# A decoder trunk whose transposes of FFN activations and residual chunks move from TensorE to VectorE and a trip through DRAM

## The chip, the cores and the metric

The kernel runs on 1 core of one Trainium2 chip. The metric is the device time of one execution in microseconds (us), lower is better; each time given for the kernel is the median of several runs. The profile is one further execution, taken by the hardware profiler.

## The reference

Two layers over 256 positions of width 2048, all in float32. Each layer has a mixing half and an FFN half:

```
h = rmsnorm(x, norm_mix);  z = h @ w_in                  # 2816 columns: q, k, v, SSM, two gMLP parts
y = concat(rmsnorm(attention), rmsnorm(SSM), rmsnorm(gMLP))
x = x + y @ w_out                                        # 2048 x 2048
h = rmsnorm(x, norm_ffn)
x = x + (silu(h @ w_gate) * (h @ w_up)) @ w_down         # D_FF = 5632
```

A final RMSNorm follows the last layer.

## The kernel before

**Matrix products.** Both operands of the large products are split into a high part (rounded to TensorE's fp32r) and a low part (the rest), and a product is three matmuls: high x high, high x low weight, low x high weight (`unit`, lines 279 to 281). The 256 positions are two blocks of 128 (`m`), so one `unit` (one slice of 128 along the contracted dimension, 512 output columns) is six matmuls of 128x128 by 128x512, with the activations as the stationary operand. These must stand transposed in SBUF: 128 features on the partitions, 256 positions along the free dimension. `X` (tiles xh, xl: 16 slices) holds the normalised input, `Y` (tiles ya and yb: 8 slices each, high and low) the mixer outputs or the FFN activations.

**The weight stream.** `stream_plan` lists all weight pieces in the order of use; each is read as two halves of 128x1024, 512 KB (`pump`, line 178, on SP's DMA queue, five raw buffers). A half is two units. ScalarE copies it into the high part (`split_hi`, line 187) and VectorE subtracts to get the low part (`split_lo`, line 197), into four buffers each. `take_half` keeps the high split up to three halves and the low split up to two halves ahead of the matmuls. A raw buffer is free again when its low split is done, and only then does SP issue the load that takes its place.

**The order of the work.** The program is one instruction stream per engine, in an order written out by `dense`: after each unit it calls `tick`, which advances the side tasks, each a Python generator, by one step. `yield w` leaves a task out for w further ticks. So a step's place in the queues of all engines is counted in units. Where a later `dense` needs data of a side task, `ready` holds events, and `need` calls `tick` until the event is set.

**The FFN.** 11 chunks of 512 columns in sets of 4, 4 and 3 (`FF_SETS`). For each chunk there are a gate and an up product of 16 units each. `ffn_h` (line 943) takes silu of the gate, `ffn_u` (line 953) multiplies the up product into it on VectorE, and `to_T` (line 343) transposes the result [256 x 512] to four slices of `Y`: eight transposes on TensorE against an identity, in two groups of four, each into one PSUM tile ("side"); `evac_T` copies such a tile to the high part on ScalarE (line 368) and subtracts for the low part on VectorE (line 369). After the chunks of a set, its part of `w_down` follows: four output chunks n of 512 columns, 4 units for each chunk of the set.

**The residual chunks.** When an output chunk n of `w_out`, or in the last set of `w_down`, is complete, `x_chunk` adds it to x (`add_x`, line 963), waits eight ticks, transposes the chunk (line 343), scales it by the norm's gain while it splits it (lines 377 and 379), and sums its squares (`x_stats`, line 328). The gate product that follows, or the next layer's first input projection, begins with chunk 0 of `X` and comes to chunk 3 at its unit 12. The chunk that is complete last is n = 3.

**Other users of the queues.** In layer 0's FFN, `ssm_prep` computes the SSM's tables of layer 1 and saves them to DRAM (1792 KB each, SP's queue); at the start of layer 1, `ssm_load` (line 491) reads the first back, in the tick after the first unit.

Of the kernel before, what the change touches and what calls it, by code (L numbers as in the profile page):

```python
# [10 lines left out]
F32 = mybir.dt.float32  # L11
F32R = mybir.dt.float32r
AF = mybir.ActivationFunctionType
ALU = mybir.AluOpType
# [22 lines left out]
def out_tiles():  # L37
    order = [(0, 0), (0, 1), (1, 0), (1, 1), None, (0, 3), (1, 3), (0, 2), (1, 2)]
    order += [(2, k) for k in (0, 1, 3, 2)] + [(3, k) for k in (0, 1, 3, 2)]
    return order  # L40


def stream_plan():
    plan = []
    for l in range(L):
        for c in (0, C_K, 512, C_U, C_ZV, C_ZU):
            w = 256 if c == C_K else 512
            plan += [("w_in", l, k, c, w) for k in range(w // 128)]
        for t in out_tiles():
            plan += [("ssm_w_glu", l, 0, 0, 512)] if t is None else [("w_out", l, t[1], 512 * t[0], 512)]  # L50
        for s in FF_SETS:
            for c in s:
                plan += [("w_gate", l, k, 512 * c, 512) for k in range(4)]
                plan += [("w_up", l, k, 512 * c, 512) for k in range(4)]
            for n in range(4):
                plan += [("w_down", l, c, 512 * n, 512) for c in s]
    return plan


# [93 lines left out]
class Builder:  # L153
# [183 lines left out]
    def to_T(self, parts, dst, ev, k0, nb, gain):  # L337
        nc = self.nc
        for b in range(nb):
            ps = yield from self.grab("side")  # L340
            for kk in range(2):
                for m in range(2):
                    nc.tensor.transpose(ps[:, 256 * kk + 128 * m:256 * kk + 128 * m + 128],  # L343
                                        parts(2 * b + kk, m), self.ident)
            yield 0
            if b:
                ev[(k0 + 2 * b - 2) // 2]["done"] = True
            self.evac_T(ps, dst, k0 + 2 * b, gain)
            self.drop("side")
        yield 0  # L350
        ev[(k0 + 2 * nb - 2) // 2]["done"] = True

    def x_chunk(self, nrm, ev, n, gofs, l, pre=None):
        if pre is not None:
# [592 lines left out]
    def ffn_u(self, i, au, rs):  # L947
        nc = self.nc
        v = nc.vector
        g = self.gbuf  # L950
        for m in range(2):
            sl = slice(512 * m, 512 * m + 512)
            v.scalar_tensor_tensor(out=g[:, sl], in0=au[m], scalar=rs[:, m:m + 1], in1=g[:, sl],
                                   op0=ALU.mult, op1=ALU.mult)
        yield 2
        yield from self.to_T(lambda k, m: g[:, 512 * m + 128 * k:512 * m + 128 * k + 128],
                             self.Y, self.hev, 4 * i, 2, None)
        self.drop("t4")

    def add_x(self, acc, n):  # L960
# [4 lines left out]
    def build(self):  # L965
        nc = self.nc
# [42 lines left out]
        nrm = self.new_x_norm()  # L1009
        xev = self.events()  # L1010
# [16 lines left out]
        for l in range(L):  # L1027
            rs = nrm["rs"]
            ready = [xev[k // 2] for k in range(16)]
# [28 lines left out]
            a = self.acc()  # L1058
            self.dense(a, self.X, D16, ready=ready)
            self.spawn(self.attn(l, 0, a, rs))  # L1060
            a = self.acc()
            self.dense(a, self.X, D16, n=256)
            self.spawn(self.kv(a, rs))
            a = self.acc()
            self.dense(a, self.X, D16)
            self.spawn(self.attn(l, 1, a, rs))
            a = self.acc()
# [3 lines left out]
            a = self.acc()  # L1071
            self.dense(a, self.X, D16)
            self.spawn(self.gmlp_v(l, a, rs))
            a = self.acc()
            self.dense(a, self.X, D16)
            self.spawn(self.gmlp_u(l, a, rs))
            rdy = [self.yev[k // 2] for k in range(16)]
            nrm = self.new_x_norm()
            xev = self.events()
            accs, cnt = {}, {}  # L1080
            for t in out_tiles():
                if t is None:
                    self.need(tssm)
                    a = []
                    for m in range(2):
                        while self.used.get("side", 0) >= 4:
                            self.tick()
                        self.used["side"] = self.used.get("side", 0) + 1
                        a.append(self.ps.tile([128, 512], F32, tag="side", name="side", bufs=4))
                    self.dense(a, self.Y, range(8, 12))  # L1090
                    self.spawn(self.ssm_out(l, a))
                    continue
                n, kt = t
                f = n not in accs
                if f:
                    accs[n] = self.acc()
                    cnt[n] = 0
                cnt[n] += 1
                self.dense(accs[n], self.Y, range(4 * kt, 4 * kt + 4), first=f, last=cnt[n] == 4, ready=rdy)
                if cnt[n] == 4:  # L1100
                    self.spawn(self.x_chunk(nrm, xev, n, 16, l, pre=lambda n=n, ac=accs[n]: self.add_x(ac, n)))


            rs = nrm["rs"]
            ready = [xev[k // 2] for k in range(16)]
# [3 lines left out]
            for si, s in enumerate(FF_SETS):  # L1109
                self.hev = self.events()  # L1110
                for i, c in enumerate(s):
                    a = self.acc()
                    self.dense(a, self.X, D16, ready=ready)
                    tgte = self.spawn(self.ffn_h(c, i, a, None, rs))
                    a = self.acc()
                    self.dense(a, self.X, D16)
                    self.need(tgte)
                    self.spawn(self.ffn_u(i, a, rs))
                ns = 4 * len(s)
                rdy = [self.hev[k // 2] for k in range(ns)]  # L1120
                last = si == len(FF_SETS) - 1
                if last:
                    nrm = self.new_x_norm()
                    xev = self.events()
                for n in range(4):
                    a = self.acc()
                    if last and l + 1 == L and n == 3:
                        self.dense_tail(a, self.Y, range(ns))
                    else:
                        self.dense(a, self.Y, range(ns), ready=rdy)  # L1130
                    if not last:
                        def add(n=n, a=a):
                            yield 0
                            self.add_x(a, n)
                        self.spawn(add())
                    elif l + 1 < L:
                        self.spawn(self.x_chunk(nrm, xev, n, 0, l + 1, pre=lambda n=n, a=a: self.add_x(a, n)))
                    else:
                        if n == 0:
                            nf = []  # L1140
                            for i in range(2):
                                while self.used.get("t4", 0) >= 4:
                                    self.tick()
                                self.used["t4"] += 1
                                nf.append(self.work.tile([128, 1024], F32, tag="t4", name="nf", bufs=4))
                                nc.sync.dma_start(out=nf[i], in_=dr["nfin"][0:1, 1024 * i:1024 * i + 1024].to_broadcast([128, 1024]))
                            sqs = []
                            while self.used.get("t4", 0) >= 4:
                                self.tick()
                            self.used["t4"] += 1  # L1150
                            junk = self.work.tile([128, 1024], F32, tag="t4", name="junk", bufs=4)

                        def fin(m, n=n, a=a):
                            xs = self.x[:, m, 512 * n:512 * n + 512]
                            nc.vector.tensor_tensor(out=xs, in0=xs, in1=a[m], op=ALU.add)
                            nc.scalar.activation(out=junk[:, 512 * m:512 * m + 512], in_=xs, func=AF.Square,
                                                 accum_out=nrm["ss"][:, m, n:n + 1])

                        def times_nf(m, n=n):
                            xs = self.x[:, m, 512 * n:512 * n + 512]  # L1160
                            nc.vector.tensor_tensor(out=xs, in0=xs, in1=nf[n // 2][:, 512 * (n % 2):512 * (n % 2) + 512],
                                                    op=ALU.mult)

                        def fin2(fin=fin, times_nf=times_nf):
                            for m in range(2):
                                fin(m)
                                times_nf(m)
                                yield 0

                        if n < 3:  # L1170
                            self.spawn(fin2())
# [3 lines left out]
        for m in range(2):  # L1175
            r = nrm["rs"][:, m:m + 1]
            t = self.work.tile([128, 2], F32, tag="ms", name="ms", bufs=4)
# [40 lines left out]
```

## Time and profile before

| | |
|---|---|
| median of 3 runs | 2070.57 us (2070.07 to 2072.56) |
| profiled execution | 2073.87 us, its span on the core 2072.0 us |
| TensorE busy | 2041.6 us, 99% of the span, 9728 matmuls |
| VectorE busy | 1210.9 us, 58% |
| ScalarE busy | 969.9 us, 47% |
| GpSimd busy | 206.1 us, 10% |
| mean granted TensorE clock | 0.993 of 2.4 GHz |
| DMA | 387.98 MB, 187 GB/s |

PE is TensorE, PEld its weight loads (of the stationary operand), DVE VectorE, ACT ScalarE, POOL GpSimd, SP the queue that issues all DMAs here. Matmuls are pipelined: their durations overlap, and what one costs is read from the distance of the starts.

### The profile page before, as it was taken

To read this page: it belongs to the slowest core of one execution; us is meant where nothing else is said; L and a number is where in the kernel's file an instruction comes from. 1 tells how busy PE (TensorE), PEld (TensorE's weight loads), DVE (VectorE), ACT (ScalarE), POOL (GpSimd) and SP (SyncE) were. 2 spreads that over 40 slices of the span, in tenths; PEclk is the share of its full clock that TensorE was granted. 3 is DMA by queue.
4 is the path that set the end of the run, shared out by engine and by line. 5 is a ranking of instruction groups with operands and counts; after the bars stand their busy time and mean duration, and the time that the engine had idled before them with its cause. 6 is when DMAs were issued, how large, how long until landed. Compare 5 with 4: busy or idle time off the path is not lost.

```text
span 2072.0 us, 25614 instructions
## 1 busy us (share of the span) xinstructions
PE 2041.6 (99%) x9728; PEld 1708.3 (82%) x9728; DVE 1210.9 (58%) x1625; ACT 969.9 (47%) x1289; POOL 206.1 (10%) x196
## 2 busy tenths in 40 slices
PE   8998999999999999999999999999999999999998
PEld 7878888888888888888888888888888888888886
DVE  6898755646555545444556796554455444554445
ACT  6555555444444443344455445544443444434444
POOL 0455004021312100000000010000000000000000
PEclk9998999999999999999999999999999999999999
DMA  7443455566656566665565455555566555555664
GB/s 247 154 142 137 131 185 187 185 217 198 219 197 218 184 219 191 193 192 188 184 218 185 148 186 182 184 189 187 191 192 193 186 192 192 189 194 186 193 194 142
DMA packets 105595, 387.98 MB, mean 187 GB/s; under 512 B 12288, under 2 KB 13056, under 8 KB 104192
## 3 DMA queue, kind: packets, MB, share of 16 engines
q1 hardware_dynamic: 105472, 386.35, 56.8%
q8 instruction: 76, 1.25, 0.2%
q14 instruction: 47, 0.39, 0.1%
HBM read 375.03 MB, written 11.27 MB: 186 GB/s over the span
## 4 chain that ended last, share of the span: by engine, by line
PE 94%; DVE 4%; issue 1%; ACT 0%; DMA 0%; SPq 0%; POOLq 0%; POOL 0%; ACTq 0%; DVEq 0%
PE acc L279 29%; PE acc L281 29%; PE acc L280 29%; PE side L343 2%; DVE wlo L197 1%; PE side L853 1%; PE side L625 1%; PE side L817 1%; DVE st L633 0%; PE side L585 0%; PE side L842 0%; PE side L663 0%; PE side L661 0%; DMA raw<-wts 0%; PE side L658 0%
## 5 line engine op out<-in xcount | busy, mean ns | idle before, releaser
L197 DVE TENSOR_TENSOR wlo<-raw,whi 128x1024 fp32r<-128x1024 f32 (+1 forms) x687 | 855.6, 1250 | 658.9 <-ACT whi L187 657.9
L187 ACT ACTIVATE whi<-raw 128x1024 fp32r<-128x1024 f32 (+1 forms) x687 | 725.8, 1058 | 971.1 <-PE acc L281 919.2
L279 PE MATMUL acc<-whi,xh 128*128 128x512 f32 (+1 forms) x1792 | 704.2, 393 | 1.9 <-ACT whi L187 1.9
L281 PE MATMUL acc<-whi,xl 128*128 128x512 f32 (+1 forms) x1792 | 693.1, 387 | 0.0
L280 PE MATMUL acc<-wlo,xh 128*128 128x512 f32 (+1 forms) x1792 | 692.6, 387 | 0.0
L281 PEld LDWEIGHTS acc<-whi,xl 128*128 128x128 f32 x1792 | 337.6, 188 | 69.4
L279 PEld LDWEIGHTS acc<-whi,xh 128*128 128x128 f32 x1792 | 337.9, 189 | 65.4 <-ACT whi L187 2.3
L280 PEld LDWEIGHTS acc<-wlo,xh 128*128 128x128 f32 x1792 | 338.1, 189 | 63.6 <-DVE wlo L197 0.4
L279 PE MATMUL acc<-whi,ya 128*128 128x512 f32 x512 | 202.0, 394 | 0.0
L280 PE MATMUL acc<-wlo,ya 128*128 128x512 f32 x512 | 199.4, 390 | 0.8 <-DVE wlo L197 0.8
L281 PE MATMUL acc<-whi,ya 128*128 128x512 f32 x512 | 199.5, 390 | 0.0
L279 PE MATMUL acc<-whi,yb 128*128 128x512 f32 x448 | 176.4, 394 | 0.0
L281 PE MATMUL acc<-whi,yb 128*128 128x512 f32 x448 | 174.6, 390 | 0.0
L280 PE MATMUL acc<-wlo,yb 128*128 128x512 f32 x448 | 174.4, 389 | 0.0
L317 POOL TENSOR_TENSOR rs<-ms,nh 128x2 f32<-128x2 f32 (+1 forms) x12 | 12.2, 1013 | 1505.9 <-DVE ms L316 1388.0
L280 PEld LDWEIGHTS acc<-wlo,ya 128*128 128x128 f32 x512 | 96.3, 188 | 20.3 <-DVE wlo L197 1.2
L281 PEld LDWEIGHTS acc<-whi,ya 128*128 128x128 f32 x512 | 96.1, 188 | 20.3
L279 PEld LDWEIGHTS acc<-whi,ya 128*128 128x128 f32 x512 | 96.2, 188 | 19.0
L281 PEld LDWEIGHTS acc<-whi,yb 128*128 128x128 f32 x448 | 84.1, 188 | 17.7
L280 PEld LDWEIGHTS acc<-wlo,yb 128*128 128x128 f32 x448 | 84.2, 188 | 16.8
L279 PEld LDWEIGHTS acc<-whi,yb 128*128 128x128 f32 x448 | 84.1, 188 | 16.8
L379 DVE SCALAR_TENSOR_TENSOR xl<-side,gains,xh 128x256 fp32r<-128x256 f32 x64 | 27.9, 480 | 44.1 <-ACT xh L377 44.1
(223 smaller groups left out, 1280.7 us busy)
## 6 DMA issues: line engine op xcount, KB each, us to landing
raw<-wts SPq DMA_DIRECT2D x684, 512.0 KB, 4.2
saved<-stash SPq DMA_DIRECT2D x4, 1792.0 KB, 6.3
stash<-saved SPq DMA_DIRECT2D x3, 1792.0 KB, 7.6
stashb<-saved SPq DMA_DIRECT2D x2, 1792.0 KB, 8.9
bc<-bc SPq DMA_DIRECT2D x8, 256.0 KB, 4.5
out<-x SPq DMA_DIRECT2D x8, 256.0 KB, 3.0
saved<-stashb SPq DMA_DIRECT2D x1, 1792.0 KB, 7.3
x<-x SPq DMA_DIRECT2D x3, 512.0 KB, 8.2
```

What stands on the lines that cost most here:

```text
L187: self.nc.scalar.activation(out=h[:, o:o + w], in_=self.raw[j][:, o:o + w], func=AF.Copy)
L197: self.nc.vector.tensor_tensor(out=o[:, i:i + w], in0=r[:, i:i + w], in1=self.hi[j][:, i:i + w], op=ALU.subtract)
L279: nc.tensor.matmul(out=o, lhsT=a, rhs=wh, start=first, stop=False)
L280: nc.tensor.matmul(out=o, lhsT=a, rhs=wl, start=False, stop=False)
L281: nc.tensor.matmul(out=o, lhsT=b, rhs=wh, start=False, stop=last)
L317: nc.gpsimd.tensor_tensor(out=out, in0=t, in1=self.nh[:, 0:w], op=ALU.pow)
L343: nc.tensor.transpose(ps[:, 256 * kk + 128 * m:256 * kk + 128 * m + 128], parts(2 * b + kk, m), self.ident)
L379: nc.vector.scalar_tensor_tensor(out=o, in0=src, scalar=gain[:, k:k + 1], in1=h.bitcast(F32), op0=ALU.mult, op1=ALU.subtract)
L625: nc.tensor.matmul(out=ps[:, 256 * o + 64 * g:256 * o + 64 * g + 64], lhsT=st[nm][:, 128 * g:128 * g + 128], rhs=U4[:, 4 * ct + g, :])
L817: nc.tensor.matmul(out=ps[:, nk * i:nk * i + nk], lhsT=qT[:, h0 + i], rhs=self.kT[:, j, cq, 0:nk], start=(j == 0), stop=(j == 1))
L853: nc.tensor.matmul(out=ps[:, 64 * i:64 * i + 64], lhsT=pT[:, 128 * (nb * i + b):128 * (nb * i + b) + 128], rhs=self.v[:, b, 64 * cq:64 * c ...
```

## The change

The transposes of the 22 FFN activation chunks and of 12 residual chunks (four behind each layer's `w_out`, four at the layer boundary), eight for each chunk, leave TensorE. `turn_T` takes their place: VectorE transposes the 32x32 squares of the chunk; four DMAs write the result to a DRAM tile, one for each 32 partitions, in pieces of 1 KB; one DMA reads it back with the squares' rows and columns exchanged; and ScalarE and VectorE split it from SBUF. All five DMAs are on SP's queue. The input's chunks at the start and the mixer outputs keep `to_T`. `x_chunk_turned` does not wait the eight ticks. For the sets of three, `down_parts` orders the down product so that output chunks 0 and 1 take the set's first two chunks first, then its third; the weight plan follows.

```
+def down_parts(s):
+    n = len(s)
+    if n > 3:
+        return [(c, range(n)) for c in range(4)]
+    return [(0, range(n - 1)), (1, range(n - 1)), (0, [n - 1]), (1, [n - 1]), (2, range(n)), (3, range(n))]
...
-            for n in range(4):
-                plan += [("w_down", l, c, 512 * n, 512) for c in s]
+            for n, part in down_parts(s):
+                plan += [("w_down", l, s[i], 512 * n, 512) for i in part]
...
+    def turn_T(self, src, dst, ev, k0, gain):
+        nc = self.nc
+        yield from self.take("st", 2)
+        t = self.work.tile([128, 1024], F32, tag="st", name="turn", bufs=2)
+        to = t.rearrange("p (b k m i) -> p k b m i", b=4, k=4, m=2)
+        for m in range(2):
+            nc.vector.transpose(out=to[:, :, :, m], in_=src(m).rearrange("p (k b j) -> p k b j", k=4, b=4))
+        yield 1
+        d = self.dram.tile([4, 32, 4, 256], F32, tag="turned", name="turned", bufs=4)
+        for a in range(4):
+            nc.sync.dma_start(out=d[:, :, a].rearrange("b j f -> j b f"),
+                              in_=t[32 * a:32 * a + 32].rearrange("p (b f) -> p b f", b=4))
+        self.drop("st")
+        yield 2
+        yield from self.take("qT", 2)
+        q = self.work.tile([128, 1024], F32, tag="qT", name="quad", bufs=2)
+        nc.sync.dma_start(out=q, in_=d.rearrange("b j a f -> (b j) (a f)"))
+        yield 3
+        qv = q.rearrange("p (a c i) -> p c a i", a=4, c=8)
+        step = 4 if gain is None else 2
+        for c in range(0, 8, step):
+            k = k0 + c // 2
+            v = lambda o: o.rearrange("p k (m a i) -> p (k m) a i", m=2, a=4)
+            h, o = v(dst.hi(k, k + step // 2)), v(dst.lo(k, k + step // 2))
+            if gain is None:
+                nc.scalar.activation(out=h, in_=qv[:, c:c + step], func=AF.Copy)
+                nc.vector.tensor_tensor(out=o, in0=qv[:, c:c + step], in1=h.bitcast(F32), op=ALU.subtract)
+            else:
+                g = gain[:, k:k + 1]
+                nc.scalar.activation(out=h, in_=qv[:, c:c + step], func=AF.Copy, scale=g)
+                for m in range(2):
+                    nc.vector.scalar_tensor_tensor(out=o[:, m], in0=qv[:, c + m], scalar=g, in1=h[:, m].bitcast(F32),
+                                                   op0=ALU.mult, op1=ALU.subtract)
+            if c % 4 == 4 - step:
+                ev[(k0 + c // 2) // 2]["done"] = True
+        self.drop("qT")
+
+    def x_chunk_turned(self, nrm, ev, n, gofs, l, pre):
+        pre()
+        yield 0
+        yield from self.turn_T(lambda m: self.x[:, m, 512 * n:512 * n + 512], self.X, ev, 4 * n,
+                               self.gains[:, l, gofs:gofs + 16])
+        yield from self.x_stats(nrm, n)
...
-        yield 2
-        yield from self.to_T(lambda k, m: g[:, 512 * m + 128 * k:512 * m + 128 * k + 128],
-                             self.Y, self.hev, 4 * i, 2, None)
+        yield 0
+        yield from self.turn_T(lambda m: g[:, 512 * m:512 * m + 512], self.Y, self.hev, 4 * i, None)
...
-                    self.spawn(self.x_chunk(nrm, xev, n, 16, l, pre=lambda n=n, ac=accs[n]: self.add_x(ac, n)))
+                    self.spawn(self.x_chunk_turned(nrm, xev, n, 16, l, pre=lambda n=n, ac=accs[n]: self.add_x(ac, n)))
...
-                for n in range(4):
-                    a = self.acc()
+                accs = {}
+                for n, part in down_parts(s):
+                    a = accs[n] if n in accs else self.acc()
+                    fresh = n not in accs
+                    accs[n] = a
...
-                        self.dense(a, self.Y, range(ns), ready=rdy)
+                        ks = [4 * i + j for i in part for j in range(4)]
+                        self.dense(a, self.Y, ks, ready=rdy, first=fresh, last=ks[-1] == ns - 1)
+                    if part[-1] != len(s) - 1:
+                        continue
...
-                        self.spawn(self.x_chunk(nrm, xev, n, 0, l + 1, pre=lambda n=n, a=a: self.add_x(a, n)))
+                        self.spawn(self.x_chunk_turned(nrm, xev, n, 0, l + 1, pre=lambda n=n, a=a: self.add_x(a, n)))
```

## Rows read from the trace of the kernel before

**Rows 1.** The page: engines' busy us, and the granted clock in 40 slices.

```profile
PE 2041.6 (99%) x9728; PEld 1708.3 (82%) x9728; DVE 1210.9 (58%) x1625; ACT 969.9 (47%) x1289; POOL 206.1 (10%) x196
...
PEclk9998999999999999999999999999999999999999
```

**Rows 2.** The chain that ended last, shares by line.

```profile
by line: PE acc L279 29.0%; PE acc L281 28.8%; PE acc L280 28.8%; PE side L343 2.1%; DVE wlo L197 1.2%; PE side L853 0.9%; issue 0.8%; PE side L625 0.7%; PE side L817 0.5%; DVE st L633 0.5%; PE side L585 0.4%; PE side L842 0.4%; PE side L66
```

**Rows 3.** The waits: engine and line, releaser, us in total, times, longest.

```profile
ACT whi L187 <- PE acc L281: 919.2, 596, 6.2
...
ACT whi L187 <- DMA raw<-wts: 3.6, 4, 1.4
```

**Rows 4.** The timeline of PE, 1509 to 1518 us: start us, duration us, instruction.

```profile
1509.74 0.39 PE L279 MATMUL acc<-whi,ya 128*128 128x512 f32 x1
...
1514.95 0.40 PE L281 MATMUL acc<-whi,ya 128*128 128x512 f32 x1
1515.19 0.60 PE L343 MATMUL side<-ident,t 128*128 128x128 f32 x4
1515.54 0.49 PE L279 MATMUL acc<-whi,ya 128*128 128x512 f32 x1
1515.87 0.39 PE L280 MATMUL acc<-wlo,ya 128*128 128x512 f32 x1
```

**Rows 5.** Groups by line, line 343: count, busy us, mean ns, idle before.

```profile
L343 PE MATMUL side<-ident,t 128*128 128x128 f32 x224 | 32.9, 272 | 0.0
L343 PE MATMUL side<-ident,x 128*128 128x128 f32 x128 | 20.6, 287 | 5.9 <-DMA x<-x 5.9
```

**Rows 6.** Groups by line: what is nearest to the added and removed work.

```profile
L197 DVE TENSOR_TENSOR wlo<-raw,whi 128x1024 fp32r<-128x1024 f32 (+1 forms) x687 | 855.6, 1250 | 658.9 <-ACT whi L187 657.9
...
L379 DVE SCALAR_TENSOR_TENSOR xl<-side,gains,xh 128x256 fp32r<-128x256 f32 x64 | 27.9, 480 | 44.1 <-ACT xh L377 44.1
...
L369 DVE TENSOR_TENSOR ya<-side,ya 128x512 fp32r<-128x512 f32 x24 | 16.6, 692 | 30.5 <-ACT ya L368 30.5
...
L610 DVE STREAM_TRANSPOSE U<-t 128x512 f32<-128x512 f32 x4 | 2.6, 688 | 1.2 <-ACT t L606 1.2
...
L737 DVE SCALAR_TENSOR_TENSOR k<-acc,rs,k 128x128 fp32r<-128x128 f32 x8 | 2.4, 343 | 2.1 <-ACT k L734 2.1
```

**Rows 7.** The timeline of DVE, ACT and SP around the same down projection's start.

```profile
1509.46 1.40 DVE L953 SCALAR_TENSOR_TENSOR t<-acc,rs,t 128x512 f32<-128x512 f32 x2
1511.03 1.23 DVE L197 TENSOR_TENSOR wlo<-raw,whi 128x1024 fp32r<-128x1024 f32 x1 [0.17 <-ACT whi L187]
...
1512.66 1.06 ACT L187 ACTIVATE whi<-raw 128x1024 fp32r<-128x1024 f32 x1 [1.66 <-PE acc L281]
...
1512.29 0.33 SPq L178 DMA_DIRECT2D raw<-wts  x1
```

**Rows 8.** DMA issues: count, KB each, median us to landing.

```profile
raw<-wts SPq DMA_DIRECT2D x684, 512.0 KB, 4.2
saved<-stash SPq DMA_DIRECT2D x4, 1792.0 KB, 6.3
stash<-saved SPq DMA_DIRECT2D x3, 1792.0 KB, 7.6
...
out<-x SPq DMA_DIRECT2D x8, 256.0 KB, 3.0
```

**Rows 9.** Windows: stretch, engines' busy us (instructions), granted clock, DMA share, GB/s.

```profile
74.00:78.00 4.00, 1.20 (x6) 0.66 (x4) 3.96 (x6) 1.47 (x2) 3.23 (x3) 0.91 0.59 194
78.00:84.00 6.00, 5.76 (x20) 4.98 (x21) 5.66 (x20) 2.26 (x7) 0.00 (x0) 0.50 0.26 90
...
1520.00:1600.00 80.00, 80.00 (x354) 66.28 (x353) 41.39 (x39) 30.94 (x30) 0.00 (x0) 1.00 0.61 196
```

**Rows 10.** The timeline of PE and SP at the layer boundary.

```profile
1062.73 0.40 PE L279 MATMUL acc<-whi,xh 128*128 128x512 f32 x1
...
1064.86 0.42 SPq L491 DMA_DIRECT2D stash<-saved  x1
```

## The prediction

> **What bounds the kernel now.** I read the page's summary first. TensorE is busy through practically the whole span, and its granted clock is 0.9 or more of 2.4 GHz in all slices but one near the start [rows 1]. A busy TensorE alone proves little, so the chain of waits comes next: TensorE's three matmul lines make up 86.6% of the chain that ended last, the transposes' line L343 another 2.1%, VectorE's weight split L197 only 1.2% [rows 2]. The waits say who follows whom: ScalarE's weight split waits 919 us in all for TensorE to give back a buffer and only 3.6 us for a weight DMA [rows 3]. So the feeders are ahead of TensorE and held back by it. What leaves TensorE is time won, as long as no feeder falls behind.
>
> The unit of time is the matmul. From the first matmul of a down projection at 1509.74 to the one at 1514.95 are 23 steps in 5.21 us, 0.2265 us each [rows 4]. One `unit` is six of them, 1.36 us, and `tick` is called once a unit; a weight half is two units, 2.72 us.
>
> **What is removed.** 34 chunks of 8 transposes (22 FFN activation chunks, 8 residual chunks behind the output projections, 4 at the layer boundary) are 272, in 68 groups of four. What a group costs is read from the starts around it: the last matmul before it starts at 1514.95, the next at 1515.54, 0.59 us where 0.2265 is normal (+0.36), and the one after comes 0.33 later (+0.10): 0.46 us [rows 4]. The second reading is the chain: 2.1% of 2072.0 us over 384 transposes of that line (224 and 128 by the rows, and by the code 32 of the attention's output) is 0.113 us each, 0.453 a group [rows 2, 5]. The duration column, 272 ns each [rows 5], overlaps and isn't the price: four take 0.60 us from first start to last end. I take 0.453: 68 x 0.453 = 30.8 us; the other reading gives 31.3. TensorE waited for nothing at those transposes (idle 0.0 [rows 5]), so no stall goes with them.
>
> The Trainium skill (TensorE: Matmul & The Clock Gate, Part 4: PE-mode transpose) gives some 275 ns for a transpose inside a kernel. The duration column agrees, the starts don't; by it 75 us would go, and that is a rival below.
>
> **What is added, on each engine.** VectorE: two 32x32-square transposes of 128x512 a chunk, 0.688 us each by the only such row [rows 6] (sources and targets in 32-element runs there too): 34 x 1.38 = 47 us. Its low-part work on FFN chunks was 0.692 us out of PSUM [rows 6] and now reads SBUF; the weight split's 1.25 us for twice the width bounds it at 0.63 [rows 6]: no change. On residual chunks four 480 ns instructions become eight of 128x128 at 343 ns [rows 6], +0.8 us. ScalarE copies the same amount as before, by the weight split's rate (1.06 us for 128x1024 [rows 7]) 0.53 us for 128x512. In steady state VectorE needs 1.23 us of each 2.72 us [rows 7], so a burst of 2 us is absorbed by the two or three halves that they are ahead. Nothing is charged; without that lead 34 x about 2 us = 68 us would show.
>
> SP: five more DMA issues a chunk at 0.33 us each [rows 7], 1.7 us, and the read's wait for the four writes to land. Behind the waiting SP stand the weight loads. A raw load is issued some 7 halves before TensorE uses it and 4 halves (10.9 us) before ScalarE splits it (`pump`, five raw buffers and leads of 3 and 2), and lands in 4.2 us [rows 8]: SP may stand still for about 6.7 us. Bytes: 34 chunks write and read 512 KB each, 35 MB beside the 350 MB of the 684 weight loads [rows 8], on DMA engines that were busy 0.61 of a late stretch [rows 9]: hidden.
>
> **The path that can stall.** Most chunks are needed tens of us later. Seven are needed at once: the last chunk of the four sets of four, the last residual chunk before each FFN, and the last one at the layer boundary; TensorE wants them at unit 12 of the following dense. (In the two sets of three, `down_parts` puts that at unit 16, 5.4 us later.) For the set that ends at T = 1509.74: VectorE's multiplications end at T+1.1 [rows 7], the square transposes at T+2.5, the split behind them at T+3.7; SP, whose next weight load waits for that split, issues it, then the four writes, the last at about T+5.1. A landing isn't in the trace for this shape: the output stores (256 KB to DRAM) take 3.0 us, the saves of 1792 KB 6.3 [rows 8]; 512 KB is nearer the first, so 3.3: T+8.4. Then the read, as large as a weight load, 4.2 us, up to 1.5 more behind a load just issued (512 KB at the 330 GB/s that 196 GB/s at 0.61 busy implies [rows 9]): T+12.6 to T+14.1. ScalarE comes to the copies after unit 10's tick behind a weight split that waits for half 5 (T+13.6) and takes 1.06: T+14.8. With 0.6 for the high and 0.7 for the low part the data are there at T+15.4 and T+16.1. TensorE needs them at T+16.3 (12 units). It just fits. I charge 0.2 us for each of six. At the layer boundary the same tick also issues the load of the saved state, at 1064.86 [rows 10], 2.1 us after the first matmul of that layer at 1062.73 [rows 10], 7.6 us to land [rows 8] and ahead of the writes: they land near T+11.3 (2.1 + 7.6 + 1.6 for their own bytes), the read between T+15.7 and T+18.8 (two loads ahead); with 1.2 for the copy that is a stall of 0.6 to 3.7, I take 2. Stalls: 1.2 + 2 = about 3.
>
> Sum, against the profiled execution (span 2072.0, 2073.87 with what lies around it): 2073.87 - 30.8 + 3 = 2046.1. The median of the runs is 3.3 below that execution, so 2042.8, rounded to 2043. Differences under 0.2% (4.1 us) this measurement can't tell from none.
>
> **Rivals.** *Late hand-offs (0.19).* The round trip is 1 to 4 us longer than I think: writes of 1 KB pieces from 32 partitions land like the larger saves (6.3), or the read queues behind two loads. Each of the seven then stalls 1 to 3 us: 7 to 21 us, 2047 to 2061. For: no row shows such a write or a read that depends on one. Against: 512 KB is a third of a save.
>
> *Slower by the clock (0.08).* Where TensorE did only 1.20 us of work in 4, the next 6 us ran at a granted 0.50, 1.2 GHz [rows 9]. If the round trip ends so late that each hand-off waits about 3.4 us, longer than the 2.8 us idle there, and the next 6 us run at half clock (3 us lost), each loses 6.4: 7 x 6.4 = 45 us against 30.8 won: 2085. It decides from a stall of about 4.4 us alone, or from the one that drops the clock. For: the margin is about 1 us. Against: both transfers would have to take half as long again as their rows.
>
> The Trainium skill (VectorE: DVE Perf Modes, Rules for kernel authors) says to use TensorE for a full 128x128 transpose when PSUM is an acceptable target, which is what is undone here. It names no price for a trip through DRAM; no row of this trace does either.
>
> *No change (0.05).* Something else paces the stream: the freed time turns into waiting for weights, or the stalls come to 27 to 35 us. 2067 to 2074. Against: ScalarE waited for weight DMA 3.6 us in the whole run [rows 3].
>
> *The full duration goes (0.03).* If a transpose really held TensorE for its 272 ns, 272 x 0.272 = 74 us go: 1997. Against it stand the starts above.
>
> **Chances.** My forecast 0.65, with its own range 2037 (no stall, the larger saving: 2039, less the 2.5 us by which the three runs before differ) to 2048 (seven stalls of just over 1 us). Faster by over 0.2%: 0.65 + 0.19 + 0.03 = 0.87; within: 0.05; slower: 0.08. For 8 in 10 the range takes all of the first and most of the late hand-offs: 2037 to 2058.
>
> **What would show it.** Right: L343 falls from 384 transposes to 112; matmul starts stay 0.2265 apart; two transposes of about 0.69 us a chunk on VectorE; SP's wait for the written squares under 2 us each; ScalarE's splits still released by TensorE. Wrong: idle time on TensorE at the start of the down, gate and first input projections put down to the high-part copy, to the low-part subtraction or to the read of the squares; weight splits that wait for weight DMAs; new stretches at a granted 0.50.

## The result, and the profile after

The changed kernel takes 2048.11 us (median of 4 runs, 2046.47 to 2049.39) where the kernel before took 2071.57 beside it (2070.07 to 2073.86): ratio 0.9887 [0.9876, 0.9899], 23.5 us faster. The forecast was 2043, its wide range 2037 to 2058, its own range 2037 to 2048: the sign is right, and the time lies inside the wide range and 0.1 us beyond the forecast's own. The forecast was worked out from a median before of 2070.57, as 27.8 us won (30.8 - 3); 23.5 were, so some 4 us of the gain are missing. (In one execution of a later experiment, the one with both delays mended, the granted clock was 0.625; its 3013.64 us are left out of the median there.)

The page of the changed kernel's profiled execution (span 2045.2 us) answers to [rows 1]: busy us, share of the span and instructions of each engine, then the granted clock in 40 slices.

```profile
PE 2012.2 (98%) x9456; PEld 1681.9 (82%) x9456; DVE 1251.7 (61%) x1741; ACT 968.6 (47%) x1289; POOL 211.0 (10%) x196
...
PEclk9998999999999999999999999999999999999999
...
PE 90%; DVE 6%; DMA 2%; issue 1%; ACT 1%; SPq 0%; POOLq 0%; POOL 0%; ACTq 0%; DVEq 0%
```

TensorE has 272 instructions less, VectorE 40.8 us of work more. The last line is the chain that ended last, by engine: VectorE holds 6% of it and DMAs 2% (4% and 0% before), so at some places TensorE now follows them. A slice of 51 us is too long to show the fall of the clock that comes below. The groups by line show what left and what came (against [rows 5, 6]; columns as there):

```profile
L351 PE MATMUL side<-ident,t 128*128 128x128 f32 x48 | 6.5, 272 | 0.0
L351 PE MATMUL side<-ident,x 128*128 128x128 f32 x32 | 6.3, 331 | 5.0 <-DMA x<-x 5.0
L351 PE MATMUL side<-ident,yattn 128*128 128x128 f32 x32 | 5.5, 311 | 0.0
...
L368 DVE STREAM_TRANSPOSE turn<-t 128x512 f32<-128x512 f32 x44 | 28.5, 685 | 0.0
...
L393 DVE SCALAR_TENSOR_TENSOR xl<-quad,gains,xh 128x128 fp32r<-128x128 f32 x96 | 26.3, 348 | 32.5 <-ACT xh L391 32.5
...
L388 DVE TENSOR_TENSOR ya<-quad,ya 128x512 fp32r<-128x512 f32 x24 | 16.1, 710 | 28.5 <-ACT ya L387 28.5
L387 ACT ACTIVATE ya<-quad 128x512 fp32r<-128x512 f32 x24 | 13.7, 618 | 4.2 <-DMA quad<-turned 4.2
```

The transposes' line keeps 48 + 32 + 32 = 112. The squares (685 ns) and the low parts (348, 710) came out as priced, ScalarE's copies at 618 rather than 530 ns. DMA issues (count, KB each, median us to landing; against [rows 8]):

```profile
raw<-wts SPq DMA_DIRECT2D x684, 512.0 KB, 4.3
turned<-turn SPq DMA_DIRECT2D x136, 128.0 KB, 4.0
quad<-turned SPq DMA_DIRECT2D x34, 512.0 KB, 4.9
```

Each leg of the trip is 0.7 us above its estimate (3.3 and 4.2). The waits (engine and line, releaser, us in total, times, longest; against [rows 3]):

```profile
ACT whi L195 <- PE acc L289: 872.8, 544, 6.2
...
SPq L378 <- DMA turned<-turn: 36.0, 41, 4.7
...
ACT whi L195 <- DMA raw<-wts: 22.3, 13, 2.9
...
ACT xh L391 <- DMA quad<-turned: 12.1, 7, 4.1
...
PE acc L287 <- ACT xh L391: 4.3, 1, 4.3
```

The weight split is still released by TensorE almost always. The one long new wait of TensorE is the last line, once, 4.3 us, for the high-part copy of a residual chunk. In TensorE's own list the copies of turned FFN chunks (L387) appear once, with 0.7 us.

Most hand-offs are clean. This is the timeline of VectorE, SP and ScalarE around the down product that starts at T = 1491.47, layer 1's first set (start us, duration, instruction):

```profile
1491.19 1.40 DVE L1006 SCALAR_TENSOR_TENSOR t<-acc,rs,t 128x512 f32<-128x512 f32 x2
1492.51 1.29 DVE L368 STREAM_TRANSPOSE turn<-t 128x512 f32<-128x512 f32 x2
...
1495.31 1.89 SPq L372 DMA_DIRECT2D turned<-turn  x4
...
1500.19 0.33 SPq L378 DMA_DIRECT2D quad<-turned  x1
...
1506.45 1.15 ACT L387 ACTIVATE yb<-quad 128x512 fp32r<-128x512 f32 x2
```

Multiplied by T+1.1, squares by T+2.3, writes issued by T+5.7, read issued at T+8.7 (so the writes had landed), copies from T+15.0 where T+14.8 was forecast. TensorE did not wait there.

The layer boundary is the exception. Here T, the first matmul of layer 1, is 1044.11; lines from the timelines of these engines, the idle time before and its releaser in brackets:

```profile
1044.11 0.39 PE L287 MATMUL acc<-whi,xh 128*128 128x512 f32 x1
...
1046.07 1.71 ACT L391 ACTIVATE xh<-quad,gains 128x256 fp32r<-128x256 f32 x4 [3.42 <-DMA quad<-turned]
...
1046.62 2.19 DVE L393 SCALAR_TENSOR_TENSOR xl<-quad,gains,xh 128x128 fp32r<-128x128 f32 x8 [5.42 <-ACT xh L391]
1048.72 1.22 DVE L205 TENSOR_TENSOR wlo<-raw,whi 128x1024 fp32r<-128x1024 f32 x1
1049.86 1.28 DVE L1015 TENSOR_TENSOR x<-x,acc 128x512 f32<-128x512 f32 x2
...
1042.04 8.32 SPq L186 DMA_DIRECT2D raw<-wts  x3
1050.40 0.43 SPq L544 DMA_DIRECT2D stash<-saved  x1
...
1054.14 1.83 SPq L372 DMA_DIRECT2D turned<-turn  x4
...
1061.72 0.33 SPq L378 DMA_DIRECT2D quad<-turned  x1
...
1065.48 1.71 ACT L391 ACTIVATE xh<-quad,gains 128x256 fp32r<-128x256 f32 x4 [4.08 <-DMA quad<-turned]
...
1066.04 0.79 PE L287 MATMUL acc<-whi,xh 128*128 128x512 f32 x1 [4.30 <-ACT xh L391]
...
1079.68 0.45 PE L829 MATMUL side<-identr,q 128*128 128x128 f32 x4
```

Read it from the top. Chunk 2's squares come back from DRAM at 1046.05. In VectorE's program chunk 2's low parts (L393) stand ahead of chunk 3's addition (L1015), and VectorE does not pass them by: it is idle for 5.42 us, then does chunk 2, a weight split, and only at T+5.8 the addition. In the clean case above, the step at this place in the trip (the multiplication) stands at T-0.3. SP, held in three weight loads from 1042.04 to 1050.36 of which the last waits for a buffer that this late split frees, comes to the saved state's load (L544) at T+6.3 where before it was T+2.1 [rows 10]; chunk 3's writes follow and have landed at T+17.6, its read is there at T+21.4. TensorE wanted the chunk at about T+16.3.

Two windows from there (stretch, length, busy us and instructions of PE, PEld, DVE, ACT, POOL, then granted clock, DMA share, GB/s):

```profile
1061.60:1064.00 2.40, 0.14 (x1) 0.00 (x0) 0.00 (x0) 0.00 (x0) 0.00 (x0) 1.00 1.04 415
1064.20:1071.00 6.80, 4.96 (x12) 3.90 (x13) 4.72 (x12) 3.88 (x9) 1.61 (x1) 0.50 0.47 187
```

From 1064.20 on, still within the stall, the granted clock is 0.50, 1.2 GHz, for 6.8 us. TensorE works in 4.96 us of them, so half of that, some 2.5 us, is what the clock costs. The price of the whole place is read from one stretch of identical work, the layer's first matmul to its first transpose of a query (L829): 35.57 us here (1044.11 to 1079.68), 27.84 in a kernel below that does not stall there, with both delays mended:

```profile
1045.01 0.39 PE L287 MATMUL acc<-whi,xh 128*128 128x512 f32 x1
...
1072.85 0.37 PE L829 MATMUL side<-identr,q 128*128 128x128 f32 x3
```

That is 7.7 us, where 2 were charged: 4.3 for the stall, some 2.5 for the clock, and the rest in small delays, of which the longest is a wait of 0.49 us for a late weight half.

### The profile page after: what moved, and what is told of

It is laid out like the page before. It is cut to its first block, busy times and chain, and to the rows that moved or that the text cites. A ratio compares the mean times of both kernels' runs of the same rounds, so it can differ in the third digit from the quotient of the medians.

```text
span 2045.2 us, 25410 instructions
## 1 busy us (share of the span) xinstructions
PE 2012.2 (98%) x9456; PEld 1681.9 (82%) x9456; DVE 1251.7 (61%) x1741; ACT 968.6 (47%) x1289; POOL 211.0 (10%) x196
## 4 chain that ended last, share of the span: by engine, by line
PE 90%; DVE 6%; DMA 2%; issue 1%; ACT 1%; SPq 0%; POOLq 0%; POOL 0%; ACTq 0%; DVEq 0%
PE acc L287 28%; PE acc L289 28%; PE acc L288 28%; DVE wlo L205 2%; DMA turned<-turn 1%; PE side L906 1%; PE side L678 1%; PE side L351 1%; DMA quad<-turned 1%; PE side L870 1%; DVE st L686 0%; PE side L638 0%; PE side L895 0%; PE side L716 0%; PE side L714 0%
## 5 line engine op out<-in xcount | busy, mean ns | idle before, releaser
L393 DVE SCALAR_TENSOR_TENSOR xl<-quad,gains,xh 128x128 fp32r<-128x128 f32 x96 | 26.3, 348 | 32.5 <-ACT xh L391 32.5
```

Of the source, the lines that this page charges most:

```text
L393: nc.vector.scalar_tensor_tensor(out=o[:, m], in0=qv[:, c + m], scalar=g, in1=h[:, m].bitcast(F32), op0=ALU.mult, op1=ALU.subtract)
```

## Experiments

Each time stands against the kernel before on the same chip. The first four were made on this theory: at the boundary two delays add up, the late addition and the state's load ahead of the writes.

**The state's load later**, 14 units into layer 1:

```
-                    preps[(l, ct)] = self.spawn(self.ssm_load(l, ct) if l else self.ssm_prep(l, ct), delay=23 * l * ct)
+                    preps[(l, ct)] = self.spawn(self.ssm_load(l, ct) if l else self.ssm_prep(l, ct), delay=(23 * ct or 14) if l else 0)
```

> The load of the saved state at the layer boundary is issued 14 ticks later, after the last chunk's read of its squares; all else as changed. In the changed kernel TensorE stalls 4.3 us there and runs 6.8 us at half clock (3.4 us lost), 7.7 us in all. Theory (two delays add up: the chunks before come late and hold ScalarE and VectorE, and the load of 1792 KB stands ahead of the last chunk's writes; either alone would nearly fit): stall under 1.5 us, no half clock, about 2041. Rival 1 (the load alone): stall 0, 2040.4. Rival 2 (the crowded chunks alone): stall still above 3 us with the half clock, 2047 to 2048.

(The half clock cost some 2.5 us by the window above, not 3.4; that 4.3 and 3.4 add up to 7.7 is chance.)

Measured 2045.96 against 2070.82, 0.9881 [0.9867, 0.9896]. The stall stayed. In its timeline the addition is nearly as late as before, T+4.8 instead of T+5.8 (T = 1045.46):

```profile
1050.27 1.28 DVE L1015 TENSOR_TENSOR x<-x,acc 128x512 f32<-128x512 f32 x2
...
1066.30 0.79 PE L287 MATMUL acc<-whi,xh 128*128 128x512 f32 x1 [4.15 <-ACT xh L391]
```

The load is not the main delay, and neither is the sum: the late addition alone is enough.

**Chunks 0 and 1 of the boundary back on TensorE**:

```
-                        self.spawn(self.x_chunk_turned(nrm, xev, n, 0, l + 1, pre=lambda n=n, a=a: self.add_x(a, n)))
+                        chunk = self.x_chunk if n < 2 else self.x_chunk_turned
+                        self.spawn(chunk(nrm, xev, n, 0, l + 1, pre=lambda n=n, a=a: self.add_x(a, n)))
```

> The residual chunks 0 and 1 of the layer boundary, whose trips overlap in the changed kernel, go back to TensorE (16 transposes, 1.8 us); the load of the saved state stays where it was. Theory (two delays add up): stall under 1.5 us, no half clock, 2048.1 - 7.7 + 1 + 1.8 = about 2043. Rival 1 (the load alone): the stall stays near 4 us with the half clock, about 2050. Rival 2 (the crowded chunks alone): stall 0, 2042.

Measured 2050.77 against 2070.82, 0.9898 [0.9882, 0.9914]. That is the time of rival 1, the load alone; but with the load out of the way, in the run above, the stall stayed all the same. It stays here too (T = 1047.00):

```profile
1048.26 2.19 DVE L393 SCALAR_TENSOR_TENSOR xl<-quad,gains,xh 128x128 fp32r<-128x128 f32 x8 [4.18 <-ACT xh L391]
...
1051.50 1.28 DVE L1015 TENSOR_TENSOR x<-x,acc 128x512 f32<-128x512 f32 x2
...
1067.73 0.50 PE L287 MATMUL acc<-whi,xh 128*128 128x512 f32 x1 [4.24 <-ACT xh L391]
```

So it isn't the number of chunks under way: chunk 2 alone, ahead of chunk 3, is enough.

**Chunk 3 of the boundary back on TensorE** (`n == 3` in the same line):

> Only the last residual chunk of the layer boundary goes back to TensorE (8 transposes, 0.9 us). If the whole loss of 7.7 us hangs on this one hand-off: no stall, no half clock near 1060, 2048.1 - 7.7 + 0.9 = 2041.3. If the half clock there has another cause than the stall: 2044.7, with a granted 0.50 still in the profile there. If the stall merely moves to the chunks before: 2045 to 2048.

Measured 2042.46 against 2070.82, 0.9869 [0.9853, 0.9886]: 28.4 us won with 33 of the 34 chunks, and no wait of TensorE for a residual copy. The boundary's loss hangs on that one hand-off.

**Load late, and chunk 1's steps spread** over four more units, in all residual hand-offs (the load's line as above):

```
         pre()
-        yield 0
+        yield 4 if n == 1 else 0
```

> The load 14 ticks later as in the first run, and chunk 1 of every residual hand-off waits 4 ticks more before its squares are turned, so that its trip begins 8 units after chunk 0's instead of 4. Theory (two delays add up): stall 0 at the boundary, ScalarE's waits for the read of the squares of the residual chunks fall from 12.1 us to under 6, 2040.4; against the first run 0 to 1 us. Rival 1 (the load alone): the same as the first run. Rival 2 (the crowded chunks alone): clearly below the first run, by 4 us or more.

Measured 2049.45 against 2070.82, 0.9896 [0.9882, 0.9911]: no better than with the late load alone, where all three expectations named the same time or a shorter one. In TensorE's waits for residual copies there are three where there was one:

```profile
PE acc L287 <- ACT xh L391: 4.5, 3, 2.1
```

Behind layer 0's `w_out` chunk 1's copies, moved back, now end 1.1 us before chunk 2's addition starts (296.89 and 297.94 in the timeline), 3.5 us in the changed kernel (288.21 and 291.68), and stalls appeared there too. My first theory had fallen; the new one is VectorE's order: copies that wait for a DMA stand in front of the addition on which the last chunk's trip depends.

**Chunk 2's copies held back** by four units at the boundary, nothing else, so that chunk 3's addition stands ahead of them:

```
-        yield 3
+        yield 3 + hold
...
-                               self.gains[:, l, gofs:gofs + 16])
+                               self.gains[:, l, gofs:gofs + 16], hold=4 if gofs == 0 and n == 2 else 0)
```

> The changed kernel, with the copies of the layer boundary's residual chunk 2 issued 4 ticks later, so that the last chunk's add and squares stand ahead of them in VectorE's queue. New theory (chunk 2's late read holds VectorE, the last chunk's add starts 4.5 us late, and the whole last trip with it): the add at about 1 us after the layer's first matmul instead of 5, the stall at unit 12 falls from 4.3 to 0.6 to 3.5 us (the state's load still stands ahead of the writes), mostly without the half clock: 2041 to 2045. Rival (the read waits behind the weight loads in the one DMA queue, whenever the trip starts): the stall stays at 4 us with the half clock, 2046 to 2049.

Measured 2043.51 against 2071.86, 0.9862 [0.9848, 0.9877]. Its timeline (T = 1045.74), and the window from the stall on:

```profile
1045.45 1.28 DVE L1015 TENSOR_TENSOR x<-x,acc 128x512 f32<-128x512 f32 x2
...
1050.15 2.19 DVE L393 SCALAR_TENSOR_TENSOR xl<-quad,gains,xh 128x128 fp32r<-128x128 f32 x8 [1.09 <-ACT xh L391]
...
1062.73 0.50 PE L287 MATMUL acc<-whi,xh 128*128 128x512 f32 x1 [0.52 <-ACT xh L391]
```
```profile
1062.00:1071.00 9.00, 8.48 (x48) 7.29 (x48) 6.75 (x15) 7.05 (x13) 1.61 (x1) 1.00 0.59 200
```

The addition is back at T-0.3, the stall is 0.52 instead of 4.30 us, and the clock stays at 1.00 (the window). The order on VectorE is the cause. (The edit holds ScalarE's copies back as well, but the addition and the squares are VectorE's alone, and so is the weight split that SP waited for.) With the state's load still ahead of the writes, 0.5 us are left, just under the 0.6 to 3.7 forecast for that.

**Both: copies held and load late.**

> As the run with chunk 2's copies 4 ticks later, and the load of the saved state 14 ticks later too. New theory: nothing is late any more, stall under 1 us, 2040 to 2042. Rival (the queue behind weight loads): stall 2 to 4 us as with the later load alone, 2044 to 2047.

Measured 2040.46 (2040.21 to 2042.68) against 2071.86, 0.9853 [0.9833, 0.9873]. The boundary no longer stalls: both delays exist, and the load's is the small one. The stretch of 27.84 us shown with the result is from here.

**The price of a transpose**: the kernel before, with the same 272 transposes issued twice.

```
-                    nc.tensor.transpose(ps[:, 256 * kk + 128 * m:256 * kk + 128 * m + 128],
-                                        parts(2 * b + kk, m), self.ident)
+                    for _ in range(times):
+                        nc.tensor.transpose(ps[:, 256 * kk + 128 * m:256 * kk + 128 * m + 128],
+                                            parts(2 * b + kk, m), self.ident)
...
+                             times=1 if l == 0 and gofs == 0 else 2)
...
+                             self.Y, self.hev, 4 * i, 2, None, times=2)
```

> The kernel before, with each of the 272 transposes issued twice (the second writes the same values again). Theory (a transpose costs the distance of the starts, 0.113 us): 272 x 0.113 = 30.8 us slower, or 24 if a longer run of transposes costs less at its edges (0.35 of the 0.46 us of a group). Rival (the duration, 0.272 us, is the price): 74 us slower.

Measured 2099.98 against 2071.86, 1.0135 [1.012, 1.015]: 28.1 us for 272 more (24.9 to 31.1 by the interval), 0.103 each: between the 24 and the 30.8 that were expected, and far from 74. The duration, from the groups by line:

```profile
L344 PE MATMUL side<-ident,t 128*128 128x128 f32 x400 | 52.0, 272 | 0.0
```

The FFN chunks' 176 among them, now issued twice, still show 272 ns each. The Trainium skill (TensorE: Matmul & The Clock Gate, Part 4: PE-mode transpose) gives some 275 ns in one kernel's context, beside a figure for bf16. The 272 ns of float32 here agree with that as a duration; by the 0.103 us it is not what a transpose costs in this stream.

**The five DMAs of a trip on ScalarE's queue** instead of SP's (`nc.scalar.dma_start`), so that they wait behind no weight load's issue:

> The changed kernel with all five DMAs of each trip issued by ScalarE instead of SP, so in another queue than the weight loads. Rival (the one DMA queue, where writes and read stand behind 512 KB loads): the write lands in about 3.3 us instead of 4.0, the read in 4.2 instead of 4.9, the stall at the boundary goes below 2 us and that of 0.7 us at 507 goes: 2040 to 2043. New theory (VectorE's order at the boundary): the trips are shorter everywhere, but the boundary keeps 2 us or more: 2043 to 2046. If ScalarE's wait for the writes holds its weight splits instead: TensorE waits for high parts, above 2050.

Measured 2050.11 against 2071.86, 0.9896 [0.9881, 0.991]. DMA issues, then waits:

```profile
turned<-turn ACTq DMA_DIRECT2D x136, 128.0 KB, 4.3
quad<-turned ACTq DMA_DIRECT2D x34, 512.0 KB, 4.9
```
```profile
ACT whi L195 <- DMA raw<-wts: 51.8, 31, 3.1
...
ACT whi L195 <- DMA turned<-turn: 9.5, 2, 6.2
...
PE acc L287 <- ACT xh L391: 4.7, 1, 4.7
```

The trip is no shorter, the stall the same, and now ScalarE's weight splits wait behind the DMAs, though TensorE waits for a high part no longer than in the changed kernel (1.4 us). The time is the changed kernel's within the scatter, above what the new theory named. The rival, SP's queue as the boundary's cause, falls. The Trainium skill (DMA: Bandwidth & Descriptors, Issuing engines are not separate DMA queues) says that DMAs share the same DMA engines whoever starts them; the landings here agree (4.3 and 4.9 us from ScalarE's queue, 4.0 and 4.9 from SP's).

**Only the FFN chunks turned**; all residual chunks by `x_chunk` on TensorE:

> Only the 22 FFN chunks leave TensorE; all 12 residual chunks are transposed there as before, 8 ticks after they are complete. 44 groups of four at 0.453 us are 19.9 us, less 0.5 to 2 us for the stall at 507: 2071.5 - 19 = 2052 to 2053.5. If the half clock and the boundary's stall belong to the FFN part after all: 2058 to 2060.

Measured 2052.44 against 2070.78, 0.991 [0.9895, 0.9925]: 18.3 us. By 0.113 us the 176 transposes of the 22 FFN chunks are 19.9. By the medians, the 12 residual chunks bring some 5 of their 10.9 us in the changed kernel; the boundary's loss covers the rest.

**Three raw buffers instead of five** in the changed kernel (`NRAW, NH = 3, 4`), against the cover that was put to SP's wait:

> The changed kernel with three raw weight buffers instead of five. Theory (the raw buffers are what hides SP's wait for the writes; three leave about 1.3 us of the 6.7): weight splits wait for weight DMAs at nearly every chunk, TensorE stalls 1 to 3 us at each of 34: 2080 to 2150. Rival (SP's wait is hidden by something else, or too short to matter): within 5 us of the changed kernel, 2043 to 2053.

Measured 2051.51 against 2070.78, 0.9904 [0.9887, 0.992]; the theory was far off, its rival right. In the waits:

```profile
ACT whi L195 <- DMA raw<-wts: 145.7, 80, 6.0
```

ScalarE waits for weights 145.7 us in all instead of 22.3, and TensorE gets its halves in time all the same. So the fourth and the fifth raw buffer are not what covers SP's wait. The split halves that stand ready ahead of TensorE may be; no run shows that.

**The writes issued twice**, first to a second DRAM tile that nobody reads: how much later may the squares come?

```
+        d0 = self.dram.tile([4, 32, 4, 256], F32, tag="first", name="first", bufs=4)
+        for to_d in (d0, d):
+            for a in range(4):
+                nc.sync.dma_start(out=to_d[:, :, a].rearrange("b j f -> j b f"),
+                                  in_=t[32 * a:32 * a + 32].rearrange("p (b f) -> p b f", b=4))
```

> The changed kernel with the four writes of each trip issued twice, first to a second DRAM tile that nobody reads: 512 KB and four issues more on each trip. Theory (the hand-offs at unit 12 have about 1 us to spare): each trip is about 2 us longer, each of the other six tight hand-offs stalls 0.5 to 2 us, the boundary 2 us more: 5 to 14 us above the changed kernel, 2053 to 2062. Rival (there is more to spare, and only the boundary's order matters): under 3 us more, 2048 to 2051.

Measured 2077.93 against 2070.78, 1.0031 [1.0019, 1.0043]: the gain is gone and 7 us with it, far above what I expected. TensorE's waits, and one window behind `w_out`:

```profile
PE acc L287 <- ACT xh L393: 12.7, 3, 6.4
PE acc L288 <- DVE wlo L205: 9.8, 9, 2.4
...
PE acc L287 <- ACT yb L389: 5.2, 4, 1.9
```
```profile
338.90:345.80 6.90, 5.85 (x14) 4.65 (x15) 4.79 (x12) 4.20 (x10) 2.93 (x4) 0.51 0.32 116
```

The four FFN hand-offs lose 5.2 us; the residual ones lose 12.7 in three stalls, of 3.9, 6.4 and 2.3 us. Against the changed kernel, that is some 13 us more at the hand-offs, within the 5 to 14 of the theory. What it had not seen are the weight halves that come late nine times, 9.8 us against 1.0, and the clock: it stands at half in the stretch shown, again for 6.8 us at the boundary and for 3.4 us shortly before, where TensorE works in some 14 us in all, about 7 lost against 2.5 there. The outcome, slower than before, is that of the rival "slower by the clock". Its mechanism is the smaller part: TensorE's matmul lines wait 29.1 us in all against 7.4.

**The best version found**: copies held, load late, and the order of `down_parts` that the sets of three had for the sets of four too:

```
-    if n > 3:
-        return [(c, range(n)) for c in range(4)]
```

> The version with chunk 2's copies and the state's load later, and the sets of four in the down order of the sets of three too, so that a set's last activation chunk is needed 12 units later. Theory (only hand-offs with too little time stall): the 0.4 to 1.8 us stall at 507 goes too, 0 to 2 us below the version without it: 2039.5 to 2041.5 where the kernel before takes 2071.5. Rival (that stall comes from layer 0's table work on VectorE and not from the time the trip has): no difference, 2041.6.

Measured 2038.24 (2037.08 to 2039.47) against 2070.78, 0.9841 [0.9826, 0.9856]: 32.5 us won, the fastest version here. That is just below the range expected. Nothing in TensorE's waits is a turned chunk any more; its longest wait in the matmul lines, 1.4 us for the high part of a weight half, is one that the changed kernel had too.

## Why the prediction was right, and what it mis-sized

**The 272 transposes: right.** 0.453 us for a group of four gave 30.8 us. Doubling them costs 28.1 (24.9 to 31.1), and the versions that lose nothing at the boundary win 28.4 (33 chunks, 29.9 by the same price, less 0.3 at one set of four), 31.4 (both delays mended) and 32.5 (29.8 to 36.0 by its interval). The rival of the full duration falls.

**VectorE's work: right as a sum, wrong as an order.** Nothing was charged for its 47 us of squares, and nothing in TensorE's waits names them. But the prediction priced VectorE by busy time. What it had not seen is the place in its queue: at the boundary the copies of chunk 2 wait there for a DMA while chunk 3's addition stands behind them. In the FFN the last multiplication did not stand behind such a wait in the timeline shown.

**The six hand-offs other than the boundary: right.** In the hand-off shown, the schedule held within about a unit (T+15.0 against T+14.8 at the copy), although by the medians each leg of the trip took 0.7 us longer than estimated. One of the six shows, with 0.7 us against 1.2 charged for all; its stall came out between 0.3 and 1.8 us in the runs that left its order as it was, and it is gone in the best version, where that chunk is needed 12 units later.

**The rival "late hand-offs".** Its range, 2047 to 2061, holds the measured time too, so the time alone does not choose. Its premise, a longer round trip, came true by 1.4 us; its mechanism did not: it wants 1 to 3 us at each of seven, and TensorE's waits show 4.3 at one, 0.7 at another and none at five.

**The boundary: the step that was mis-sized.** The 2 us came from the state's load ahead of the writes. That part is real and small: 0.5 us, once the addition is in time. The rest is the addition, which ends at T+7.0 instead of the T+1.1 by which the FFN's multiplication ends, and the clock that falls in the stall; together 7.7 us instead of 2. 30.8 less 7.7 and 0.7 is 22.4, measured 23.5. The half clock was held to be one rival that wants every hand-off late, by about 3.4 us each; it came at one hand-off alone, with a stall of 4.3 us. (The 4.4 us named there is the stall that would use up the gain if all seven had it, and no point at which the clock falls.) The working also took a load just issued to hold up a read by 512 KB at 330 GB/s; the row behind it, 196 at 0.61, gives 321, which moves the result by less than 0.1 us.

**SP's wait: right in effect, wrong in reason.** "Under 2 us each" holds for the mean (36.0 us in 41 waits), not the longest, 4.7. The five raw buffers given as its cover are not all needed for it: three do nearly as well (19.3 us won against 23.5, and the intervals overlap).

**The margin: as thin as forecast.** A second set of writes turned 23 us of gain into 7 of loss. Of those 30 us, 21.7 are longer waits of the matmul lines and, as an estimate from the stretches at 0.50, some 4 the clock; the rest is not accounted for.

**Open:** whether the 32.5 us of the best version, 1.7 above the 30.8, are a slightly dearer transpose or scatter; the interval holds both.

## What to carry to other kernels

Where an engine's queue takes data from a DMA, ask what stands behind that wait, not only how long the engine is busy: 5 us of an idle VectorE cost TensorE some 7 us, the 47 us of squares added to VectorE nothing that shows. Price an instruction in TensorE's stream by the distance of starts, or by issuing it twice, not by its duration. A stall of several us on TensorE is dearer than itself when the clock falls with it, so the few hand-offs needed at once are worth an order of their own. 32 of the 34 chunks went through DRAM here without a wait of TensorE that shows.

## What was not expected of the hardware

In a stall of 4.30 us on TensorE, 1.8 us before its end, a stretch of 6.8 us at a granted 0.50, 1.2 GHz, began; after the stall of 0.52 us at the same place the clock stayed at 1.00. The length of the stall alone does not decide it: a stall of 4.24 us (chunks 0 and 1 on TensorE) was followed by 3.4 us at 0.50, one of 2.09 us (load late, chunk 1 spread) by as much, and ones of 2.37 and 2.31 us (writes twice) by none. The writes, four DMAs of 128 KB in 1 KB pieces, landed in 4.0 us each (median) and the read of 512 KB behind them in 4.9, for 34 chunks under a weight stream that goes on; with a second set of writes just ahead of them the medians were 3.4 and 5.5.
